# Attention-bias tables of an encoder layer: written whole to DRAM, or kept in place in SBUF

## The chip, the cores and the metric

One core of a Trainium2 chip runs the whole program. The metric is device time in microseconds (us) of one execution, the median of several runs. Engines are named as in the profile: PE (TensorE, matmuls) and PEld (its weight loads), DVE (VectorE), ACT (ScalarE), POOL (GpSimd), SP (SyncE, which here only issues transfers); "SPq" and "ACTq" are the transfers that SyncE and ScalarE issue.

## The reference

One encoder layer is applied to two inputs with the same weights: a sample of 1024 tokens and a prompt of 256. Width is 1024, the feed-forward width 2816, all in float32:

```python
x = x + 0.5 * rmsnorm(swiglu(rmsnorm(x, ffn1_pre), ffn1_w_gu, ffn1_w_down), ffn1_post)
h = rmsnorm(x, mix_pre)
qa, ka, va, qb, kb, vb = split(h @ w_in)
oa = window_gqa(rope(qa), rope(ka), va, sink_a)       # A: 8 heads, keys within 128 tokens
ob = neighbourhood_attn(qb, kb, vb, rpb_b)            # B: 8 heads on a (rows x 64) token grid
mix = concat([rmsnorm(oa, out_norm_a), rmsnorm(ob, out_norm_b)]) @ w_out
x = x + rmsnorm(mix, mix_post)
x = x + 0.5 * rmsnorm(swiglu(rmsnorm(x, ffn2_pre), ffn2_w_gu, ffn2_w_down), ffn2_post)
return rmsnorm(x, final_norm)
```

In `neighbourhood_attn` a query at row r and column c of the grid sees a window of at most 8 rows by 16 columns, clamped at the edges, and each score gets a learned bias `rpb[head, row difference, column difference]`; scores outside the window are set to -1e30 before the softmax.

## The kernel before, in words

**Order of the work.** The first feed-forward part is a gate-up phase (class `GateUp`) and a down phase (`Down`, `down_phase`); then come the mixer (`mix_attention`: input projection, attention A, attention B), the output projection (`MixOut`), and the second feed-forward part by the same two classes. Both feed-forward products use seven products of half-size operands instead of eight, so sums and differences of weights and of activations are formed beside the matmuls. Every float32 operand is split into a high and a low part (`split`, L65: ACT copies, DVE or POOL subtracts), and each product is three matmuls.

**Gate-up.** 22 blocks f of 128 hidden columns, in `GateUp.steps`. A block has 14 steps: seven products j for the first chunk of tokens (ch 0, 256 columns), seven for the second (ch 1, 384). PE works on a step while DVE and ACT take the step before out of PSUM (the tiles u, v, w, g) and split the next block's weights (`prep`). Results go to DRAM as planes w and v, stored by ACT. From block 11 on (`f >= HF`), the planes of block f - 11 are read back (`fetch`, tile `back`), and POOL forms four sums of old and new planes (`sums`, L328 to L338, tiles `back` and `sums`), which ACT stores. All stores are in ACT's queue, in the order written out by `queued`.

**Weights' sums.** `Down.weight_sums(i)` (L391) loads three blocks of `w_down`, forms four sums on POOL (L402 to L405, tiles `bx`, `bt`) and has ACT store them a block later. `block_hooks` puts it behind step 8 of a block; which block is told by its last argument. In the first feed-forward part that is block 1 and every even block (`f // 2 if f == 1 or f % 2 == 0`), in the second blocks 1 to 11 (`f - 1 if f <= HF`).

**Bias tables.** `bias_tables` (L518) prepares the bias of attention B in DRAM. `skew(g, tau)` puts the bias of four heads and one of three column cases tau in skewed form, with -1e30 outside the valid columns (tile `z`, POOL), and writes it to `zd` and `zp`. For the sample, `fill(a, rh)` then builds a full table `tt` out of it, from DRAM to DRAM: one transfer copies the valid band of 8 of 12 key rows for query row a and half rh, and one or two more fill the rest with the constant `neg`. For the prompt, `fill_neg` and `fill_p` build `ttp`. The list `first` (six skews, five fills) runs behind step 6 of gate-up blocks 2 to 10; the list `later` (eleven fills, four `fill_p`) is spread by `pinned` over the first three head groups of attention A, each behind the last half swap of the rope (`qs`) on SyncE's queue.

**Attention A.** Four head groups j, ten units t each (`att_A`): scores on PE (`s_ps`, out of the stacked rotated queries `stk`), a fused bias, mask and minimum on DVE (`bias_max`), exponentials on ACT, normalisation on POOL, transposes (`pt`) and the product with the values (`o_ps`) on PE, a fold on ACT and DVE into `st` (two buffers), and a store to `oAd` by SyncE. A unit's steps are spread over six steps of a software pipeline (`Pipe`, the lags in `ATT`), and the input projection of the next head group (L636, `pj`) is laid between them. Rope: ACT copies the projection (`qf`), SyncE swaps halves of its partitions (`qs`, four transfers of 32 partitions), POOL and DVE combine, and a split gives `stk`.

**Attention B.** Eight heads h, units n in the order 0, 3, 4, 1, 2 (4 is the prompt). `load_tab(h, tau)` (L857) loads a head's table: one transfer of 384 KB for tau 0 to 2 (tile `tab`, three buffers), two of 128 KB for the prompt (`tabp`). The first head's four are loaded ahead of the loop; the next head's are issued right behind the `bias_max` that read the buffer last. On SyncE's queue stand also the moves of keys to the other half of the partitions (L644, `stk`) and the loads of projection weights (L586, `mraw`), which the next heads need.

Of the kernel before, what the change touches and what calls it, by code (L numbers as in the profile page):

```python
# [19 lines left out]
NFF = FF // 128  # L20
# [146 lines left out]
class GateUp:  # L167
# [160 lines left out]
    def sums(self, f, ch):  # L328

        n, e, sub, add = CN[ch], self.c.nc.gpsimd.tensor_tensor, ALU.subtract, ALU.add  # L330
        x, y = self.back.pop((f, ch)), self.G.tile([128, 2 * n], F32, name="sums", tag=("ga", "gb")[ch], bufs=1)
        (w0, v0), (s3, s4) = [[z[:, :n], z[:, n:]] for z in (x, y)]
        w1, v1 = self.X["w"], self.X["v"]
        e(s3, w0, v0, op=sub)
        e(v0, v0, v1, op=add)
        e(w0, v0, w0, op=sub)
        e(s4, w1, w0, op=sub)
        return [lambda: self.store(("s2", "s1"), f, ch, x), lambda: self.store(("s3", "s4"), f, ch, y)]  # L338
# [41 lines left out]
class Down:  # L380
# [48 lines left out]
    def load_h(self, n):  # L429

        if n >= len(self.seq) or n in self.sub:
            return
        c, nc = self.c, self.c.nc
        q, p, m = self.seq[n]
        ch = 0 if p < CHUNKS[0][1] else 1
        k = len(PIECES[m])

        def tile(name):
            if n == 0:
                return self.G.tile([128, 6, 128], F32R, name=name, tag="x", bufs=3)[:, :k]  # L440
            return self.hp.tile([128, 6, 128], F32R, name=name, bufs=3)[:, :k]

        lo, hi = tile("hl"), tile("hh")
        g = next(g for g in PLANES if DOWN7[q][0] in g)
        src = self.hd[g][m][ch][g.index(DOWN7[q][0]) * CN[ch] // 128 + p - CHUNKS[ch][0]]
        self.last_h = nc.sync.dma_start(lo.bitcast(F32), src)
        split(c, hi, lo, lo.bitcast(F32))
        self.sub[n] = hi, lo
# [66 lines left out]
            self.cms.pop().__exit__(None, None, None)  # L515


def bias_tables(c, G, rpb, cmask, neg, tt, ttp, zd, zp):  # L518

    nc = c.nc
    def rows(g):
        rp = c.small.tile([96, 63], F32, name="rp", bufs=1)
        nc.gpsimd.memset(rp, 0.0)
        for h in range(4):
            nc.sync.dma_start(rp[h * 24 + 4:h * 24 + 19, 16:47], rpb[4 * g + h])
        nc.gpsimd.tensor_scalar(rp, rp, 8.0, None, op0=ALU.mult)
        return rp  # L530

    rps = {}

    def skew(g, tau):
        if tau == 0:
            rps[g] = rows(g)
        cm = G.tile([96, 16, 32], F32, name="cm", tag="t", bufs=2)
        nc.sync.dma_start(cm.rearrange("p q j -> p (q j)"), cmask[:, tau * 512:(tau + 1) * 512].to_broadcast([96, 512]))
        x = rps[g][:, 31 - 8 * tau:63 - 8 * tau]
        x = bass.AP(tensor=x.tensor, offset=x.offset, ap=[list(x.ap[0]), [-1, 16], [1, 32]])  # L540
        z = G.tile([96, 16, 32], F32, name="z", tag="t", bufs=2)
        nc.gpsimd.tensor_tensor(z, x, cm, op=ALU.add)
        for x in (zd[:, tau], zp[tau]):
            nc.sync.dma_start(x[:, 4 * g:4 * g + 4].rearrange("q h d j -> (h d) q j"), z)

    zf = zd.rearrange("q t h d j -> q (t h) (d j)")
    tf = tt.rearrange("t h a q r e j -> q (t h) a r (e j)")

    def fill(a, rh):
        e0 = min(a, 4) if rh else max(a - 4, 0)  # L550
        d0 = e0 - a - 4 * rh + 11
        nc.sync.dma_start(tf[:, :, a, rh, e0 * 32:e0 * 32 + 256], zf[:, :, d0 * 32:d0 * 32 + 256])
        for lo, hi in ((0, e0), (e0 + 8, 12)):
            if hi > lo:
                n = (hi - lo) * 32
                src = bass.AP(tensor=neg.tensor, offset=neg.offset, ap=[[0, 16], [0, 24], [1, n]])
                nc.sync.dma_start(tf[:, :, a, rh, lo * 32:hi * 32], src)

    def fill_p(a, n):
        nc.sync.dma_start(ttp[a, n, :, :, :, KC0[n]:KC0[n] + 32].rearrange("x h e j -> (x h) e j"),  # L560
                          zp[TAU[n], :, :, 11 - a:15 - a, :].rearrange("x h e j -> (x h) e j"))

    def fill_neg(a):
        nc.sync.dma_start(ttp[a].rearrange("n q h e k -> (n q h) (e k)"), neg.to_broadcast([512, 256]))

    first = [lambda tau=tau, g=g: (skew(g, tau), fill_neg(2 * g + tau - 1) if tau else None) for g in range(2) for tau in range(3)]
    first.append(lambda: fill(0, 0))
    fills = [lambda a=a, rh=rh: fill(a, rh) for a in range(8) for rh in range(2)][1:]
    while len(first) < HF - 2:
        two, fills = fills[:2], fills[2:]  # L570
        first.append(lambda two=two: [f() for f in two])
    return first, fills + [lambda a=a: [fill_p(a, n) for n in range(4)] for a in range(4)]

# [24 lines left out]
    return hi, lo, parts()  # L598


def mix_attention(c, tc, xt, w_in, sink, cosT, sinT, maskA, tt, ttp, oAd, oBd, mw, L, R,
                  close_left, open_out, late, mr, pre, fills):
    nc = c.nc
    xh, xl = xt
    pipe = c.pipe = Pipe()
# [96 lines left out]
    def rope(th, ps, store):  # L702
        n = TH[th][1]
        p0 = TH[th][0] % 1024
        qf = pa.tile([128, n], F32, name="qf", tag="qf", bufs=2)
        nc.scalar.activation(qf, ps, AF.Copy)
        qs = pa.tile([128, n], F32, name="qs", tag="qs", bufs=2)
        for b in range(4):
            state["pin"] = nc.sync.dma_start(qs[b * 32:b * 32 + 32], qf[(b ^ 1) * 32:(b ^ 1) * 32 + 32])
        yield  # L710
        nc.gpsimd.tensor_tensor(qf, qf, cos[:, p0:p0 + n], op=ALU.mult)
        nc.vector.tensor_tensor(qs, qs, sin[:, p0:p0 + n], op=ALU.mult)
        yield
        nc.vector.tensor_tensor(qf, qf, qs, op=ALU.add)
        yield
        store(th, qf, qs)
# [138 lines left out]
    tabs = {}  # L855

    def load_tab(h, tau):  # L857
        if h < 8:
            if tau < 3:
                T = pb.tile([128, 2, 384], F32, name="tab", bufs=3)  # L860
                nc.sync.dma_start(T.rearrange("p r x -> p (r x)"), tt[tau, h].rearrange("a q r e j -> (a q) (r e j)"))
            else:
                T = pb.tile([128, 2, 256], F32, name="tabp", bufs=1)
                for b in range(2):
                    nc.sync.dma_start(T[:, b], ttp[2 * b:2 * b + 2, :, :, h].rearrange("a n x e c -> (a n x) (e c)"))
            tabs[h, tau] = T

    def att_B(h, n, reload):

# [17 lines left out]
        rsum = c.small.tile([128, 2], F32, name="rsum")  # L887
        for i in range(2):
            bias_max(sbs[i], ps[i], tabs[h, tau][:, i, :], negm[:, i:i + 1], 3e38)
        if reload:  # L890
            load_tab(h + 1, tau)
        softmax_exp(sbs, negm, rsum)
        yield
        normalize(sbs, rsum)
        yield
        if n < 4:
# [62 lines left out]
                out.append((cost, lambda n=n, f=f: (load_to(n), f())))  # L959
        return out  # L960

    def pinned(f):
        with tc.issue_after(state["pin"].ins):
            f()

    with in_order(tc, mybir.EngineType.DVE):
        load_to(10)
        for i in (0, 16, 8):
# [9 lines left out]
    for j in range(4):  # L978
        units = [[(att_A(j, t), ATT)] for t in range(NT)]
        if j < 3:  # L980
            todo = P(("qA", j + 1))
            for n in range(7):
                if fills:
                    todo.insert(4 * n + 3, (0.0, lambda f=fills.pop(0): pinned(f)))
            pipe.run(units, todo)
        else:
            pipe.run(units + [[]] * 5, P(("qkB", 0), ("vB", 1)))
    R.close()
    pb = R.open("mixB", 1)
    for tau in (0, 2, 3, 1):  # L990
        load_tab(0, tau)
    during = [[("qkB", 1)], [("qkB", 2)], [("qkB", 3)], [("vB", 2), ("qkB", 4)], [("qkB", 5)], [("vB", 3), ("qkB", 6)], [("qkB", 7)]]
    for h in range(8):
        units = []
# [176 lines left out]
def encoder(tc, i, out_p, out_s):  # L1171
# [24 lines left out]
    oAd = dram.tile([4, 128, 1280], F32, name="oAd")  # L1196
    oBd = [dram.tile([4, 128, n], F32, name=f"oBd{n}") for n in (1024, 256)]
    zd = dram.tile([16, 3, 8, 24, 32], F32, name="zd")
    tt = dram.tile([3, 8, 8, 16, 2, 12, 32], F32, name="tt")
# [23 lines left out]
    def block_hooks(gu, f, extra, sums):  # L1223
# [19 lines left out]
        if f == NFF - 1:  # L1243
            for n, i in ((0, 0), (1, 1), (2, 2), (3, 3), (7, 4), (8, 5), (9, 6), (11, 7), (12, 8), (13, 9)):
                also(n, lambda i=i: d.load_w(0, i))
            also(12, lambda: d.load_h(0))
        return hooks

    def down_phase(gu, res, post, nxt, finish, last):
# [126 lines left out]
    for _ in nxt:  # L1376
        pass
    gu.load(2)
    late, later = bias_tables(c, G, i["rpb_b"][0], i["cmask"], i["neg"], tt, ttp, zd, zp)

    def behind():
        with tc.issue_after(gu.last_load.ins):
            late.pop(0)()

    for f in range(1, NFF):
        gu.run(f, block_hooks(gu, f, {6: behind} if 1 < f < HF else {}, f // 2 if f == 1 or f % 2 == 0 else None))
    L.close(2)
    R.close()
    state = dict(xn={}, late=[])
# [28 lines left out]
    def finish1(t, x, gain, halves, ss):  # L1418
# [7 lines left out]
        if "xt" in state:  # L1426
# [7 lines left out]
            else:  # L1434
# [9 lines left out]
    mix_attention(c, tc, state["xt"], i["w_in"][0], i["sink_a"], i["cosT"], i["sinT"], i["maskA"], tt, ttp, oAd, oBd,  # L1444
                  mw, L, R, lambda: L.close(4), mo.open, lambda: [list(x) for x in state["late"]], state["mr"], state["pre"], later)
    c.ps.use(y=(2, 3, 4, 5), tr=(6, 7, 0, 1))


# [127 lines left out]
```

## Time and profile before

| | |
|---|---|
| median of three runs | 2405.97 us (2403.55 to 2409.6) |
| the profiled execution | 2403.19 us, of which the span shown is 2401.4 |
| PE busy | 2273.8 us, 95% |
| DVE, ACT, POOL busy | 1458.6, 982.4, 709.0 us (61, 41, 30%) |
| mean granted TensorE clock | 0.977 |
| gate-up 1 / down 1 | about 20 to 610 / 610 to 890 us |
| attention A / attention B | about 959 to 1165 / 1170 to 1400 us |
| gate-up 2 / down 2 | about 1560 to 2113 / 2122 to 2390 us |

A line of the profile names engine, source line, operation, result tile and operands (`out<-in`). "Idle before" and the rows of the waits say what ended the time in which an engine stood still. A transfer's time to land runs from its issue to its last byte. The granted clock is the share of full speed that TensorE was given; below 1, the same matmuls take longer.

### The profile page before, as it was taken

What the parts mean: (1) busy time and instruction counts of PE and PEld (TensorE: products, weight loads), DVE (VectorE), ACT (ScalarE), POOL (GpSimd) and SP (SyncE); (2) the same over time, 40 slices, a digit from 0 to 9 for tenths busy, and PEclk for the clock granted to TensorE, in tenths of its full rate; (3) what the DMA queues carried; (4) which work ended last, traced back from release to release, by engine and by line L of the source; (5) the groups of instructions that cost most, each with busy time, mean ns of one, the idle gap of its engine ahead of it and who ended that gap; (6) DMA issues with size and microseconds to landing.
All of it is one profiled execution on the core that took longest, in us unless ns stands there. A gap on an engine that the chain in (4) does not pass through costs nothing. (4 is left out here: it accounts for less than half of the span.)

```text
span 2401.4 us, 36895 instructions
## 1 busy us (share of the span) xinstructions
PE 2273.8 (95%) x13328; PEld 2072.3 (86%) x13328; DVE 1458.6 (61%) x2575; ACT 982.4 (41%) x2043; POOL 709.0 (30%) x812
## 2 busy tenths in 40 slices
PE   6999999999999999878999989899999999999997
PEld 5999999999788787657898878789999999978876
DVE  7666656655545763548665656566666656544585
ACT  5322222222434543547665655342322222243454
POOL 6121125444000123436443334622213332300022
PEclk9999999999999999878999999899999999999999
DMA  4466656666656653334433445435455655555574
GB/s 135 119 155 158 153 144 195 188 184 185 208 188 192 221 184 107 73 77 85 111 106 93 123 156 176 155 114 164 139 172 157 185 145 159 149 189 183 191 230 157
DMA packets 417094, 372.47 MB, mean 155 GB/s; under 512 B 69200, under 2 KB 339408, under 8 KB 416912
## 3 DMA queue, kind: packets, MB, share of 16 engines
q1 hardware_dynamic: 286224, 278.87, 39.5%
q10 hardware_dynamic: 130688, 91.25, 12.4%
q8 instruction: 105, 1.72, 0.3%
q14 instruction: 77, 0.63, 0.1%
HBM read 249.85 MB, written 121.90 MB: 155 GB/s over the span
## 5 line engine op out<-in xcount | busy, mean ns | idle before, releaser
L280 PE MATMUL gups<-xh,ah 128*128 128x256 f32 (+1 forms) x2464 | 764.9, 311 | 18.6 <-DVE v L289 13.5
L280 PE MATMUL gups<-xh,al 128*128 128x256 f32 (+1 forms) x2464 | 762.1, 310 | 0.0
L280 PE MATMUL gups<-xl,ah 128*128 128x256 f32 (+1 forms) x2464 | 761.8, 309 | 0.0
L462 PE MATMUL dps<-wd,hh 128*128 128x512 f32 x1540 | 482.4, 394 | 7.9 <-ACT hh L69 7.9
L280 PEld LDWEIGHTS gups<-xh,ah 128*128 128x128 f32 x2464 | 466.7, 189 | 24.5 <-DVE v L289 15.8
L280 PEld LDWEIGHTS gups<-xl,ah 128*128 128x128 f32 x2464 | 467.3, 190 | 0.0
L280 PEld LDWEIGHTS gups<-xh,al 128*128 128x128 f32 x2464 | 466.9, 190 | 0.0
L462 PEld LDWEIGHTS dps<-wd,hh 128*128 128x128 f32 x1540 | 290.9, 189 | 70.3 <-ACT hh L69 9.8
L462 PE MATMUL dps<-wd,hl 128*128 128x512 f32 x770 | 304.2, 395 | 6.6 <-DVE hl L72 6.2
L69 ACT ACTIVATE ah<-s 128x512 fp32r<-128x512 f32 x176 | 111.3, 632 | 244.4 <-PE gups L280 165.9
L72 DVE TENSOR_TENSOR al<-s,ah 128x512 fp32r<-128x512 f32 x176 | 145.0, 824 | 98.1 <-ACT ah L69 97.4
L69 ACT ACTIVATE hh<-hl 128x768 fp32r<-128x768 f32 (+1 forms) x140 | 110.6, 791 | 209.6 <-DMA hl<-hd0s 55.3
L72 DVE TENSOR_TENSOR hl<-hl,hh 128x768 fp32r<-128x768 f32 (+1 forms) x140 | 124.6, 891 | 106.3 <-ACT hh L69 106.3
L462 PEld LDWEIGHTS dps<-wd,hl 128*128 128x128 f32 x770 | 145.8, 189 | 44.2 <-DVE hl L72 12.6
L659 POOL TENSOR_TENSOR sb<-sb,rc 128x384 f32<-128x384 f32 (+1 forms) x160 | 126.1, 810 | 158.0 <-DVE rc L657 144.3
L636 PE MATMUL pj<-xh,mh 128*128 128x512 f32 (+1 forms) x432 | 162.9, 378 | 0.3
L636 PE MATMUL pj<-xh,ml 128*128 128x512 f32 (+1 forms) x432 | 156.8, 363 | 0.1
L636 PE MATMUL pj<-xl,mh 128*128 128x512 f32 (+1 forms) x432 | 156.3, 362 | 0.0
L306 ACT ACTIVATE u<-u 128x256 f32<-128x256 f32 x88 | 41.5, 472 | 253.4 <-DVE u L289 208.9
L69 ACT ACTIVATE ah<-raw 128x512 fp32r<-128x512 f32 x132 | 83.4, 632 | 138.4 <-PE gups L280 131.5
L72 DVE TENSOR_TENSOR wd<-rawd,wd 128x512 fp32r<-128x512 f32 x154 | 106.2, 692 | 47.0 <-ACT wd L69 46.5
L162 POOL TENSOR_SCALAR rs<-ssq 128x1 f32<-128x1 f32 x20 | 12.5, 624 | 396.1 <-ACT junk L479 396.1
(183 smaller groups left out, 3680.4 us busy)
## 6 DMA issues: line engine op xcount, KB each, us to landing
raw<-in_ffn_w_gu_dram SPq DMA_DIRECT2D x88, 512.0 KB, 4.1
rawd<-in_ffn_w_down_dram SPq DMA_DIRECT2D x66, 256.0 KB, 3.3
bx<-in_ffn_w_down_dram SPq DMA_DIRECT2D x22, 512.0 KB, 5.1
bt<-in_ffn_w_down_dram SPq DMA_DIRECT2D x44, 256.0 KB, 4.8
rawd<-td0T SPq DMA_DIRECT2D x44, 256.0 KB, 3.2
rawd<-td1T SPq DMA_DIRECT2D x44, 256.0 KB, 3.2
tab<-tt SPq DMA_DIRECT2D x24, 384.0 KB, 3.8
hl<-hd0s SPq DMA_DIRECT2D x20, 384.0 KB, 3.2
```

The lines of the kernel that those rows point to most:

```text
L69: nc.scalar.activation(hi, src, AF.Copy)
L72: (lo_eng or nc.vector).tensor_tensor(lo, src, hi.bitcast(F32), op=ALU.subtract)
L162: nc.gpsimd.tensor_scalar(r, sums[0], sums[1] if len(sums) == 2 else 0.0, EPS, op0=ALU.add, op1=ALU.add)
L280: nc.tensor.matmul(ps, w[:, k, :], x[:, k, :], start=new and k == 0 and m == 0, stop=k == 3 and m == 2, skip_group_check=not new)
L306: self.last_act = nc.scalar.activation(X["u"], X["u"], AF.Silu)
L462: nc.tensor.matmul(ps, a[:, k, :], b, start=i == 0 and v == 0, stop=i == HF - 1 and v == 2)
L636: state["mm"] = nc.tensor.matmul(ps[:, :n], w[:, kk, :], xs[th][:, kk, :], start=first, stop=last)
L659: nc.gpsimd.tensor_tensor(s, s, rc[:, i:i + 1].to_broadcast(list(s.shape)), op=ALU.mult)
```

## The change

- The table `tt`, the function `fill` and all its transfers are removed, as is `pinned` with the fills in attention A. `bias_tables` returns one list of ten: six skews and the four `fill_p`, run behind step 6 of blocks 2 to 11.
- Attention B has three tiles `table`, one for each tau, which stay in place. POOL sets them to -1e30 once. `load_tab` writes only the valid bands, straight from `zd`: for each of eight query rows a and two halves rh, one transfer to 16 partitions with 1 KB each, so 16 transfers of 16 KB a table. It is a generator: the transfers of a = 0 to 3 are issued behind `bias_max`, those of a = 4 to 7 a pipeline step later, ahead of `normalize`. For head 0, the transfers with rh = 1 are issued by ACT; all others by SyncE.
- The first feed-forward part takes its weights' sums in blocks 1 to 11, like the second.
- Buffers: `cm` and `z` of the skew move from the slots `t` to `ga` and `gb`. The high half of the down phase's first operand (`hh` of `load_h(0)`) moves from slot `x` to `gb`, and `load_h(0)` from step 12 to step 10 of the last block; the last block's second `sums` tile moves from `gb` to `ga`. These three hold for both feed-forward parts.

```diff
     def sums(self, f, ch):
-        x, y = self.back.pop((f, ch)), self.G.tile(..., name="sums", tag=("ga", "gb")[ch], bufs=1)
+        x, y = self.back.pop((f, ch)), self.G.tile(..., name="sums", tag=("ga", "gb")[ch and f < NFF - 1], bufs=1)
...
         def tile(name):
             if n == 0:
-                return self.G.tile([128, 6, 128], F32R, name=name, tag="x", bufs=3)[:, :k]
+                t, b = ("x", 3) if name == "hl" else ("gb", 1)
+                return self.G.tile([128, 6, 128], F32R, name=name, tag=t, bufs=b)[:, :k]
...
-    first.append(lambda: fill(0, 0))
-    fills = [lambda a=a, rh=rh: fill(a, rh) for a in range(8) for rh in range(2)][1:]
-    while len(first) < HF - 2:
-        two, fills = fills[:2], fills[2:]
-        first.append(lambda two=two: [f() for f in two])
-    return first, fills + [lambda a=a: [fill_p(a, n) for n in range(4)] for a in range(4)]
+    return first + [lambda a=a: [fill_p(a, n) for n in range(4)] for a in range(4)]
...
     def load_tab(h, tau):
-        if h < 8:
-            if tau < 3:
-                T = pb.tile([128, 2, 384], F32, name="tab", bufs=3)
-                nc.sync.dma_start(T.rearrange("p r x -> p (r x)"), tt[tau, h].rearrange("a q r e j -> (a q) (r e j)"))
...
+        T = tabs[h, tau] = table[tau]
+        src = zd[:, tau, h].rearrange("q d j -> q (d j)")
+        for a in range(8):
+            if a == 4:
+                yield
+            for rh in range(2):
+                e0 = min(a, 4) if rh else max(a - 4, 0)
+                d0 = e0 - a - 4 * rh + 11
+                (nc.scalar if rh > h else nc.sync).dma_start(T[a * 16:a * 16 + 16, rh, e0 * 32:e0 * 32 + 256], src[:, d0 * 32:d0 * 32 + 256])
...
             bias_max(sbs[i], ps[i], tabs[h, tau][:, i, :], negm[:, i:i + 1], 3e38)
-        if reload:
-            load_tab(h + 1, tau)
+        load = load_tab(h + 1, tau) if reload else iter(())
+        next(load, None)
         softmax_exp(sbs, negm, rsum)
         yield
+        for _ in load:
+            pass
         normalize(sbs, rsum)
...
         if j < 3:
-            todo = P(("qA", j + 1))
-            for n in range(7):
-                if fills:
-                    todo.insert(4 * n + 3, (0.0, lambda f=fills.pop(0): pinned(f)))
-            pipe.run(units, todo)
+            pipe.run(units, P(("qA", j + 1)))
...
+    table = [pb.tile([128, 2, 384], F32, name=f"tab{x}", bufs=1) for x in range(3)]
+    for x in table:
+        nc.gpsimd.memset(x, NEG)
     for tau in (0, 2, 3, 1):
-        load_tab(0, tau)
+        for _ in load_tab(0, tau):
+            pass
...
-            also(12, lambda: d.load_h(0))
+            also(10, lambda: d.load_h(0))
...
-        gu.run(f, block_hooks(gu, f, {6: behind} if 1 < f < HF else {}, f // 2 if f == 1 or f % 2 == 0 else None))
+        gu.run(f, block_hooks(gu, f, {6: behind} if late and f > 1 else {}, f - 1 if f <= HF else None))
```

More of the change, by code (lines that the diff above doesn't have):

```diff
@@ L330, in sums @@
         n, e, sub, add = CN[ch], self.c.nc.gpsimd.tensor_tensor, ALU.subtract, ALU.add
-        x, y = self.back.pop((f, ch)), self.G.tile([128, 2 * n], F32, name="sums", tag=("ga", "gb")[ch], bufs=1)
+        x, y = self.back.pop((f, ch)), self.G.tile([128, 2 * n], F32, name="sums", tag=("ga", "gb")[ch and f < NFF - 1], bufs=1)
         (w0, v0), (s3, s4) = [[z[:, :n], z[:, n:]] for z in (x, y)]
@@ L515, in close, with bias_tables @@
             self.cms.pop().__exit__(None, None, None)
-def bias_tables(c, G, rpb, cmask, neg, tt, ttp, zd, zp):
+def bias_tables(c, G, rpb, cmask, neg, ttp, zd, zp):
     nc = c.nc
@@ L536, in skew @@
             rps[g] = rows(g)
-        cm = G.tile([96, 16, 32], F32, name="cm", tag="t", bufs=2)
+        cm = G.tile([96, 16, 32], F32, name="cm", tag="ga", bufs=1)
         nc.sync.dma_start(cm.rearrange("p q j -> p (q j)"), cmask[:, tau * 512:(tau + 1) * 512].to_broadcast([96, 512]))
@@ L540, in skew @@
         x = bass.AP(tensor=x.tensor, offset=x.offset, ap=[list(x.ap[0]), [-1, 16], [1, 32]])
-        z = G.tile([96, 16, 32], F32, name="z", tag="t", bufs=2)
+        z = G.tile([96, 16, 32], F32, name="z", tag="gb", bufs=1)
         nc.gpsimd.tensor_tensor(z, x, cm, op=ALU.add)
@@ L544, in skew @@
             nc.sync.dma_start(x[:, 4 * g:4 * g + 4].rearrange("q h d j -> (h d) q j"), z)
[L546 to L557, printed above, removed]
     def fill_p(a, n):
@@ L598, in split_win, with mix_attention @@
     return hi, lo, parts()
-def mix_attention(c, tc, xt, w_in, sink, cosT, sinT, maskA, tt, ttp, oAd, oBd, mw, L, R,
-                  close_left, open_out, late, mr, pre, fills):
+def mix_attention(c, tc, xt, w_in, sink, cosT, sinT, maskA, zd, ttp, oAd, oBd, mw, L, R,
+                  close_left, open_out, late, mr, pre):
     nc = c.nc
@@ L708, in rope @@
         for b in range(4):
-            state["pin"] = nc.sync.dma_start(qs[b * 32:b * 32 + 32], qf[(b ^ 1) * 32:(b ^ 1) * 32 + 32])
+            nc.sync.dma_start(qs[b * 32:b * 32 + 32], qf[(b ^ 1) * 32:(b ^ 1) * 32 + 32])
         yield
@@ L857, in load_tab @@
     def load_tab(h, tau):
-        if h < 8:
-            if tau < 3:
-                T = pb.tile([128, 2, 384], F32, name="tab", bufs=3)
-                nc.sync.dma_start(T.rearrange("p r x -> p (r x)"), tt[tau, h].rearrange("a q r e j -> (a q) (r e j)"))
[L862 to L865, printed above, removed]
-            tabs[h, tau] = T
+        if h >= 8:
+            return
+        if tau == 3:
+            T = pb.tile([128, 2, 256], F32, name="tabp", bufs=1)
+            for b in range(2):
+                nc.sync.dma_start(T[:, b], ttp[2 * b:2 * b + 2, :, :, h].rearrange("a n x e c -> (a n x) (e c)"))
+            tabs[h, tau] = T
+            return
+        T = tabs[h, tau] = table[tau]
[7 more added lines that the diff above has]
+                (nc.scalar if rh > h else nc.sync).dma_start(T[a * 16:a * 16 + 16, rh, e0 * 32:e0 * 32 + 256], src[:, d0 * 32:d0 * 32 + 256])
     def att_B(h, n, reload):
@@ L960, in P @@
         return out
-    def pinned(f):
-        with tc.issue_after(state["pin"].ins):
-            f()
     with in_order(tc, mybir.EngineType.DVE):
@@ L1198, in encoder @@
     zd = dram.tile([16, 3, 8, 24, 32], F32, name="zd")
-    tt = dram.tile([3, 8, 8, 16, 2, 12, 32], F32, name="tt")
     zp = dram.tile([3, 16, 8, 24, 32], F32, name="zp")
@@ L1378, in encoder @@
     gu.load(2)
-    late, later = bias_tables(c, G, i["rpb_b"][0], i["cmask"], i["neg"], tt, ttp, zd, zp)
+    late = bias_tables(c, G, i["rpb_b"][0], i["cmask"], i["neg"], ttp, zd, zp)
     def behind():
@@ L1443, in encoder @@
     c.ps.use(pj=(0, 1), s=(2, 3), t=(4, 5), o=(6, 7), y=(0, 1), tr=(6, 7))
-    mix_attention(c, tc, state["xt"], i["w_in"][0], i["sink_a"], i["cosT"], i["sinT"], i["maskA"], tt, ttp, oAd, oBd,
-                  mw, L, R, lambda: L.close(4), mo.open, lambda: [list(x) for x in state["late"]], state["mr"], state["pre"], later)
+    mix_attention(c, tc, state["xt"], i["w_in"][0], i["sink_a"], i["cosT"], i["sinT"], i["maskA"], zd, ttp, oAd, oBd,
+                  mw, L, R, lambda: L.close(4), mo.open, lambda: [list(x) for x in state["late"]], state["mr"], state["pre"])
     c.ps.use(y=(2, 3, 4, 5), tr=(6, 7, 0, 1))
```

## The prediction

> **What bounds the kernel now.** I read the page first (busy shares and the forty slices), then the stretches by stage, then who TensorE waited for in the stages with holes, then the transfers and SyncE's waits there.
>
> ```profile
> PE 2273.8 (95%) x13328; PEld 2072.3 (86%) x13328; DVE 1458.6 (61%) x2575; ACT 982.4 (41%) x2043; POOL 709.0 (30%) x812
> PE   6999999999999999878999989899999999999997
> PEclk9999999999999999878999999899999999999999
> ```
>
> TensorE is busy 95% of the span: a change can only remove its holes and the time it runs at a lowered clock, or add some. The one deep hole, in busy time and in clock, is at slices 17 to 19, which is attention A. By stage (columns: stretch, its length, busy of PE, PEld, DVE, ACT, POOL, granted clock, DMA share, GB/s):
>
> ```profile
> 100.00:350.00 250.00, 249.19 (x1710) 248.57 (x1709) 149.78 (x248) 67.03 (x128) 43.39 (x35) 1.00 0.60 154
> 350.00:607.00 257.00, 244.45 (x1652) 241.21 (x1650) 158.08 (x250) 69.36 (x134) 113.98 (x99) 0.99 0.65 187
> 959.00:997.00 38.00, 33.51 (x184) 28.47 (x184) 26.32 (x78) 25.68 (x70) 23.96 (x41) 0.91 0.30 66
> 997.00:1064.00 67.00, 45.65 (x210) 35.84 (x210) 31.61 (x90) 28.59 (x76) 21.79 (x41) 0.76 0.33 78
> 1064.00:1118.00 54.00, 44.34 (x220) 36.91 (x221) 34.36 (x92) 31.11 (x83) 23.65 (x43) 0.82 0.40 86
> 1118.00:1154.00 36.00, 35.11 (x226) 29.75 (x225) 32.78 (x98) 32.35 (x94) 26.69 (x51) 1.00 0.35 76
> 1160.00:1180.00 20.00, 20.00 (x115) 17.42 (x114) 9.23 (x26) 9.30 (x25) 6.35 (x8) 1.00 0.53 162
> 1170.00:1372.00 202.00, 201.35 (x1262) 180.45 (x1261) 127.62 (x346) 125.72 (x332) 73.66 (x98) 1.00 0.38 102
> 1600.00:1850.00 250.00, 250.00 (x1713) 250.00 (x1712) 157.99 (x255) 69.46 (x131) 59.95 (x42) 1.00 0.48 154
> 1850.00:2100.00 250.00, 250.00 (x1704) 249.67 (x1704) 150.54 (x255) 71.02 (x135) 86.09 (x85) 1.00 0.57 160
> ```
>
> Rows 3 to 6 are the four head groups j of attention A: 38, 67, 54 and 36 us for the same ten units each. Rows 1 and 2 are the halves of the first gate-up phase, the last two those of the second, which has no hole at all. Attention B (row 8) is full.
>
> **Attention A: the fills go.** Before, eleven table fills (each one copy of 384 KB and one or two fills with the constant) and four prompt fills are put into j = 0 to 2, on SyncE's queue, between the rope's half swaps (qs) and the output stores (oAd). The change takes the table fills out of the program and puts the prompt fills into gate-up blocks 8 to 11. Who TensorE waited for in j = 0 to 2, the transfers of j = 1 and then of j = 3 (last column: median us to landing), and one of SyncE's own waits:
>
> ```profile
> PE o_ps L792 <- DVE st L687: 14.2, 8, 3.6
> PE s_ps L665 <- DVE stk L72: 12.9, 7, 3.3
> ...
> oAd<-st SPq DMA_DIRECT2D x10, 64.0 KB, 7.1
> qs<-qf SPq DMA_DIRECT2D x8, 64.0 KB, 8.9
> ...
> oAd<-st SPq DMA_DIRECT2D x11, 64.0 KB, 2.2
> qs<-qf SPq DMA_DIRECT2D x1, 32.0 KB, 1.9
> ...
> SPq L799 <- DMA tt<-in_neg_dram: 4.0, 2, 3.0
> ```
>
> The reader is to see both ways in which a fill hurts. The store of `st` takes 7.1 us beside fills and 2.2 without; `st` has two buffers, so the fold waits and o_ps behind it. The half swap takes 8.9 against 1.9, so the rotated queries (stk) come late for s_ps. And SyncE stands still for a landing fill, with which store and swap share no data. Each hole then lowers the granted clock (0.76, 0.82), so the work itself stretches. The work alone is busy time by clock: 33.51 x 0.91 + 45.65 x 0.76 + 44.34 x 0.82 = 101.5 us of 159. The bounds of the gain are therefore 27 us (the first two waits, nothing else) and 57 (all idle, all clock). I take the pace of j = 3, the same code with no fill beside it: 3 x 36 = 108, a gain of **51**. It is nearer to the upper bound because DVE (31 to 34 us a group) and ACT (29 to 31) also fit in 36. Next to be late there is DVE.
>
> **First gate-up: weights' sums.** Six of the eleven weight sums (each four POOL operations) lie in blocks 1 to 10 and five in blocks 12 to 20, beside the planes' sums, also on POOL. After, all are in blocks 1 to 11, as in the second gate-up.
>
> ```profile
> PE gups L280 <- DVE v L289: 11.5, 8, 2.1
> ...
> ACT ah L69 <- POOL sums L337: 18.3, 5, 5.0
> ...
> 467.50 1.74 POOL L404 TENSOR_TENSOR bx<-bt,bx 128x512 f32<-128x512 f32 x1
> ...
> 471.61 0.74 POOL L337 TENSOR_TENSOR sums<-w,back 128x256 f32<-128x256 f32 x1
> ...
> 472.38 0.37 ACTq L319 DMA_DIRECT2D hd0s<-sums  x1
> 472.85 0.63 ACT L69 ACTIVATE ah<-s 128x512 fp32r<-128x512 f32 x1 [5.50 <-PE gups L280]
> ```
>
> The chain: weight sums (L404 is one) sit between the planes' sums (L337) on POOL, the store of the planes' sums (hd0s) waits at the head of ACT's queue until 472.38, ACT has stood 5.50 us when its next split starts (the row names TensorE, which had long been done), DVE's evacuation behind that split is late, TensorE stops. The hole of this half is 257 - 244.45 = 12.6 us; the second gate-up's same half, with no weight sums in it but for block 11, has none. Gain **12**, bounds 10 and 13. The cover in the first half: the second gate-up has a weight sum in every block at PE 250.00 of 250 and POOL 60. Here six skews come on top (before too) and four prompt fills of four transfers. I cost them at nothing; if that cover failed, the 0.8 us that this half idles now is the nearest row. The skew's new buffers (ga, gb) are last used before block 1. The hidden tile of the down phase's first load (hh, now in gb, hook 10) starts ACT's split earlier, but the hole at that seam is:
>
> ```profile
> PE dps L462 <- ACT hh L69: 2.3, 1, 2.3
> ...
> PE dps L462 <- ACT hh L69: 5.6, 1, 5.6
> ...
> 2117.20 0.99 POOL L337 TENSOR_TENSOR sums<-w,back 128x384 f32<-128x384 f32 x1
> 2118.21 0.82 SPq L446 DMA_DIRECT2D hl<-hd1w  x2
> ```
>
> The next load goes out when POOL's last sum ends, which the change doesn't move. Zero, bounds -3 and +3 (the last sum's buffer now waits for a store half a block older).
>
> **Attention B: 384 small transfers for 24 large.** Each table load (one 384 KB transfer) becomes sixteen of 16 KB. The first three tables cost three POOL memsets, 24 issues on SyncE and 24 on ACT; the other 21 cost 336 issues on SyncE, eight behind the bias step, eight a step later. The next head's k moves (stk) and weight loads (mraw) queue behind them. No row shows a 16-partition load, so its price goes by the nearest (issue time min/median/max in ns; then pairs in the order of time, us):
>
> ```profile
> L865 SPq DMA_DIRECT2D tabp<-ttp x14: 319/382/1112, 1179.9 to 1360.6; - x14
> L644 SPq DMA_DIRECT2D stk<-stk x42: 461/467/1171, 1177.0 to 1371.3; - x42
> L586 SPq DMA_DIRECT2D mraw<-in_w_in_dram x10: 383/538/723, 1170.7 to 1283.8; - x10
> ...
> 961.22 2.42 SPq L709 DMA_DIRECT2D qs<-qf  x4
> ...
> 1179.92 0.80 SPq L865 DMA_DIRECT2D tabp<-ttp  x2
> ...
> 1204.78 1.49 SPq L865 DMA_DIRECT2D tabp<-ttp  x2
> ...
> tabp<-ttp SPq DMA_DIRECT2D x14, 128.0 KB, 2.5
> ```
>
> From 0.40 us each (tabp: plain rows of 1 KB out of DRAM, as these are) to 0.605 (qs: few partitions). At 0.40: 336 x 0.40 = 134, plus what stays (42 x 0.467 + 10 x 0.538 + 14 x 0.382 = 30) is 164 of 202 us: SyncE fills 81% and TensorE's matmuls hide it. The shortest heads last 24.9 us (tabp to tabp) and take 48 x 0.40 + 5 = 24: just covered. At the start, 26 issues stand where 5 stood: 21 x 0.40 = 8.4 us; ACT's 24 (10 us) fit into its idle 10.7 of 20 at 1160. Half of the 8.4 shows: **+4**. At 0.605: 203 + 30 - 202 = 31, plus 21 x 0.605 = 13: **+44**. Below zero is excluded: TensorE idles 0.65 us there. I take +4, since tabp has source, rows and direction in common.
>
> The Trainium skill, "DMA: Bandwidth & Descriptors", section "Rules for kernel authors", speaks against this part: small transfers should be coalesced, and under 64 KB one pays mostly overhead. The page's "Anatomy of one DMA" puts that overhead at about 2.0 us a transfer (on the gpsimd path); paid one after the other, 336 of them would be an estimated 672 us, where the stage has 202. The trace agrees on the latency (tabp lands in 2.5 us), not on the sum: its pairs go out 0.40 us apart.
>
> **Sum.** 2403.2 (profiled execution) - 51 - 12 + 4 = 2344. The median of the runs is 2.8 above that execution, so 2347.
>
> **Rivals.** (1) In attention A only the direct waits go (27), the rest being the in-order chain of rope and softmax: for it, j = 2 took 54 us although its transfers were mostly the short prompt fills; against it, j = 3. 2371. (2) SyncE binds in attention B at 0.605 us: for it, all its few-partition rows; 2387. (3) Slower: the small loads don't overlap, SyncE waits for landings. It decides from 0.66 us an issue (357 x 0.66 - 172 = 63, the whole gain); at 0.70, 2421. Against it, SyncE issued six fills in 3.2 us that took 11.9 to land:
>
> ```profile
> 963.68 0.59 SPq L552 DMA_DIRECT2D tt<-zd  x1
> ...
> 966.30 0.62 SPq L557 DMA_DIRECT2D tt<-in_neg_dram  x1
> ...
> tt<-zd SPq DMA_DIRECT2D x4, 384.0 KB, 11.9
> ```
>
> With six in flight and tabp's 2.5 us to land, 0.42 is the limit. Rival 3 is what the skill's rule on small transfers would look like here.
>
> **How the numbers follow.** Forecast 0.65 (its own range 2333 to 2362); rival 1 0.16; rival 2 0.13; rival 3 0.04; 0.02 for a near tie. The range 2330 to 2382 holds forecast, rival 1 and part of rival 2. Under 0.3% (7 us) a measurement can't tell from no change: faster 0.94, same 0.02, slower 0.04.
>
> **What would show it.** Right: j = 0 to 2 at 34 to 38 us each, qs and oAd landing in about 2 us, clock near 1.00; 350 to 607 without waits of gups for v; 48 short issues a head on SyncE, 0.32 to 0.42 us each. Wrong: s_ps waiting for stk or ACT for mraw in attention B, SyncE without a gap there, ACT's exp late at its start, or j = 1 and 2 still above 45 us.

## The result: a gain of 22 us where 59 were forecast

| | before | changed |
|---|---|---|
| median of five runs | 2405.97 us (2402.64 to 2413.55) | 2384.09 us (2380.05 to 2390.71) |
| profiled execution / its span | 2403.19 / 2401.4 us | 2382.16 / 2380.4 us |

The ratio is 0.9907, 95% interval 0.9881 to 0.9933: faster, but 2384 lies just outside the range of 2330 to 2382. The page of the changed kernel, the same three lines as were shown of before:

```profile
PE 2265.4 (95%) x13328; PEld 2066.6 (87%) x13328; DVE 1457.8 (61%) x2575; ACT 980.4 (41%) x2043; POOL 713.0 (30%) x815
PE   6989999999999999999999899799999999989997
PEclk9999999999999999999999899899999999999999
```

The deep hole of slices 17 to 19 is gone. In its place PE has a dent in slice 3, early in the first gate-up phase, and one with a lowered clock at slice 23, the end of attention B. To put numbers on them, here are the rows of the timeline at which each part of the work begins, first of before (gate-up block 12, down phase, first projection, attention A, attention B, second gate-up), then of the changed kernel. The first column is the start in us.

```profile
346.94 0.28 PE L280 MATMUL gups<-xh,ah 128*128 128x256 f32 x1
...
609.80 1.05 PE L462 MATMUL dps<-wd,hh 128*128 128x512 f32 x2
...
892.18 0.48 PE L636 MATMUL pj<-xh,mh 128*128 128x512 f32 x1
...
959.10 0.50 PE L665 MATMUL s_ps<-kA,stk 128*128 128x256 f32 x2 [2.14 <-DVE stk L72]
...
1170.04 0.88 PE L665 MATMUL s_ps<-stk 128*128 128x384 f32 x4
...
1544.67 0.28 PE L280 MATMUL gups<-xh,ah 128*128 128x256 f32 x1
```

```profile
370.15 0.28 PE L280 MATMUL gups<-xh,ah 128*128 128x256 f32 x1
...
615.83 0.62 PE L463 MATMUL dps<-wd,hh 128*128 128x512 f32 x2
...
902.56 0.48 PE L619 MATMUL pj<-xh,mh 128*128 128x512 f32 x1
...
970.00 0.50 PE L648 MATMUL s_ps<-kA,stk 128*128 128x256 f32 x2 [2.14 <-DVE stk L72]
...
1121.93 0.88 PE L648 MATMUL s_ps<-stk 128*128 128x384 f32 x4
...
1521.95 0.28 PE L280 MATMUL gups<-xh,ah 128*128 128x256 f32 x1
```

Each row's lag against the same row of before, and its difference from the row ahead, gives the account:

| part | forecast | measured |
|---|---|---|
| gate-up 1 up to block 12 | 0 | **+23.2** |
| gate-up 1 from block 12 to the first down product | -12 | -17.2 |
| down 1 to the first projection | 0 | +4.4 |
| projection ahead of attention A | 0 | +0.5 |
| attention A | -51 | **-59.0** |
| attention B and output projection | +4 | **+25.4** |
| second feed-forward part | 0 | +1.7 |
| sum | -59 | -21.0 |

(Attention B and the output projection stand together, because the last units of the one run beside the first products of the other.) Two terms of the sum had the right place and came out larger than forecast, by 5 and by 8 us; that hides a part of the misses in the total. Two terms were wrong by 23 and by 21 us the other way. The stretches of the changed kernel, in the columns known from before; below them from block 12 to the first down product, and attention B with the output projection, each first before and then changed:

```profile
100.00:350.00 250.00, 235.06 (x1565) 233.79 (x1564) 153.98 (x234) 63.83 (x122) 66.44 (x47) 0.97 0.64 171
...
970.00:1004.00 34.00, 32.35 (x197) 28.09 (x198) 31.59 (x89) 28.34 (x79) 25.03 (x40) 0.95 0.23 51
1004.00:1038.00 34.00, 33.09 (x219) 29.29 (x218) 31.52 (x93) 29.69 (x84) 26.99 (x49) 1.00 0.24 55
...
1122.00:1366.00 244.00, 227.96 (x1345) 195.24 (x1343) 143.06 (x386) 140.91 (x370) 83.38 (x110) 0.97 0.40 89
```

```profile
346.94:609.80 262.86, 249.82 (x1681) 246.28 (x1681) 162.41 (x256) 71.52 (x137) 114.46 (x100) 0.99 0.64 185
370.15:615.83 245.68, 245.27 (x1682) 244.51 (x1681) 142.82 (x248) 70.46 (x133) 79.50 (x80) 1.00 0.57 159
...
1170.04:1544.67 374.63, 360.26 (x2077) 314.38 (x2076) 232.56 (x512) 218.38 (x510) 151.73 (x173) 0.98 0.43 133
1121.93:1521.95 400.02, 374.12 (x2077) 318.73 (x2076) 234.13 (x512) 220.14 (x514) 153.00 (x176) 0.96 0.44 118
```

The second half of gate-up 1 is full, as forecast. In the first half PE did 1565 matmuls in the 250 us that held 1710: it idles 14.9 us, and at a granted clock of 0.97 the work itself takes about 7.5 us longer (an estimate, 0.03 of 250). Attention A now runs at 34 us a head group. Attention B, which had been full, stands still for 16 of 244 us. Counted with the output projection, the idle time grows by 11.5 us (25.9 against 14.4), and the same 2077 matmuls are busy for 13.9 us longer, at a clock of 0.96 in place of 0.98.

**Where the first half lost its time.** Waits of the first 350 us of the changed kernel, and the time its skews' stores took to land (last column); then the same two stores before:

```profile
PE gups L280 <- ACT u L292: 14.9, 4, 4.4
...
ACT ah L69 <- DMA zd<-z: 23.0, 4, 6.1
...
zd<-z SPq DMA_DIRECT2D x6, 192.0 KB, 11.7
zp<-z SPq DMA_DIRECT2D x6, 192.0 KB, 12.5
```

```profile
zd<-z SPq DMA_DIRECT2D x6, 192.0 KB, 3.6
zp<-z SPq DMA_DIRECT2D x6, 192.0 KB, 5.5
```

Four times ACT stands still, 23.0 us in all, and four times PE waits for it. One of the four places in the timeline:

```profile
130.68 0.33 SPq L545 DMA_DIRECT2D zd<-z  x1
131.05 3.97 SPq L545 DMA_DIRECT2D zp<-z  x1
...
131.69 2.28 ACTq L406 DMA_DIRECT2D td0T<-bt  x1
...
136.54 0.33 ACTq L406 DMA_DIRECT2D td0T<-bt  x1
...
142.47 0.38 ACTq L319 DMA_DIRECT2D hd0w<-w  x1
142.90 0.63 ACT L69 ACTIVATE ah<-s 128x512 fp32r<-128x512 f32 x1 [5.32 <-DMA zd<-z]
```

The two stores of a skew (SyncE) and the three stores of the weights' sums (ACT; the first and the last are shown) go out within 6 us of each other. ACT's next plane store, `hd0w<-w`, shares no data with `zd`, but ACT comes past it only when `zd` has landed, 11.8 us after its issue, and the split behind it (`ah`) is late. In the built program the transfers of SyncE and ACT take eight completion semaphores in turn, and a transfer waits for the one eight ahead of it; here that is `zd` (in the trace, `zd<-z` and `hd0w<-w` both carry semaphore 105).

**Where attention B lost its time.** Transfers of the bands (their issue time min/median/max in ns), and SyncE's timeline at the start of the stage:

```profile
L859 SPq DMA_DIRECT2D tab<-zd x360: 302/418/1957, 1118.7 to 1356.9; - x180
...
L859 ACTq DMA_DIRECT2D tab<-zd x24: 309/432/981, 1116.6 to 1129.6; - x24
```

```profile
1118.72 16.01 SPq L859 DMA_DIRECT2D tab<-zd  x33
...
1136.62 11.79 SPq L859 DMA_DIRECT2D tab<-zd  x22
...
1165.91 11.23 SPq L859 DMA_DIRECT2D tab<-zd  x24
```

One issue takes 0.42 us, but they stand 0.47 to 0.54 us apart (11.23 / 24, 11.79 / 22). Over the stage SyncE's 360 take 187.6 us with their gaps, and hardly anything is free: from 1115 to 1366 us the gaps of over 0.3 us between its issues add up to 12.6 us (to 176 in the 240 us from 1160 of the kernel before). The next head's keys and weights come when the bands let them through.

### The profile page after: what moved, and what is told of

It reads as the page before. It is cut to its first block, busy times and chain, and to the rows that moved or that the text cites. A ratio compares the mean times of both kernels' runs of the same rounds, so it can differ in the third digit from the quotient of the medians.

```text
span 2380.4 us, 37317 instructions
## 1 busy us (share of the span) xinstructions
PE 2265.4 (95%) x13328; PEld 2066.6 (87%) x13328; DVE 1457.8 (61%) x2575; ACT 980.4 (41%) x2043; POOL 713.0 (30%) x815
## 3 DMA queue, kind: packets, MB, share of 16 engines
q10 hardware_dynamic: 131456, 91.64, 12.6%
## 5 line engine op out<-in xcount | busy, mean ns | idle before, releaser
L280 PE MATMUL gups<-xh,ah 128*128 128x256 f32 (+1 forms) x2464 | 766.8, 311 | 20.4 <-ACT u L292 14.9
L72 DVE TENSOR_TENSOR al<-s,ah 128x512 fp32r<-128x512 f32 x176 | 139.6, 793 | 107.2 <-ACT ah L69 106.5
```

What stands on the lines that cost most here:

```text
L72: (lo_eng or nc.vector).tensor_tensor(lo, src, hi.bitcast(F32), op=ALU.subtract)
L280: nc.tensor.matmul(ps, w[:, k, :], x[:, k, :], start=new and k == 0 and m == 0, stop=k == 3 and m == 2, skip_group_check=not new)
```

## The experiments

All times are medians; the gain is counted against the changed kernel's 2384. The kernel before, run again beside each group of experiments, had medians of 2403.3 to 2407.5 us, so differences of up to 4 us say nothing, and the ratios are the safer comparison. Lags and parts are each read from one profiled execution.

### 1. Which transfer stands eight behind (a_lane, a_lane4)

```diff
         for x in (zd[:, tau], zp[tau]):
             nc.sync.dma_start(x[:, 4 * g:4 * g + 4]..., z)
+        nc.sync.dma_start(c.extra[g, tau:tau + 1], z[0:1, 0])     # a_lane; in a_lane4 only if tau > 0
```

> One transfer of 128 bytes is added behind each of the six skews' two stores, nothing else. Theory (shared ring): SyncE's and ACT's transfers take eight completion semaphores in turn, and hd0w<-w stands on ACT's queue exactly eight behind zd<-z in the blocks of skews 2, 3, 5 and 6, so ACT stands still until the slow zd has landed; these are the four steps of 5 to 6 us that gate-up 1 lost (23.0 in all). By the order of this program the store stands eight behind zd in the blocks of skews 1 and 4 instead: two stalls, at those two places, 11.5 us, so 2384 - 11.5 = 2372. Rival (crowding: the skews' stores and the weights' sums' stores simply share the DMA engines, whatever the order): the four stalls stay where they are, 2384 to 2386.

> The same added transfer of 128 bytes, but only behind skews 2, 3, 5 and 6. Shared ring: no hd0w<-w stands eight behind a zd any more; the 23 us are gone but for 0 to 3, ACT has no wait for zd, 2361 to 2364, although a transfer more is issued. Crowding: 2384 to 2386, as every byte is still moved.

Measured: a_lane 2373.7, a_lane4 2376.1. The number came true for a_lane, the theory did not. ACT's wait for `zd` is gone in both, but up to block 12 they still lose 17.1 and 17.8 us instead of 23.2, in the blocks where it was lost before. ACT waits for other transfers, here in a_lane:

```profile
ACT u L306 <- DMA td0T<-bt: 26.1, 4, 7.7
...
ACT ah L69 <- DMA zp<-z: 7.5, 2, 3.9
```

The ring of eight decides which transfer ACT is seen to wait for. In these two it is worth about 6 us at block 12, and even that is not sure: four kernels with the changed kernel's code in this phase (b_two, b_pairs, b_split and e_seam, below) lag by 18.9 to 25.7 us there. The rest has another cause. (`c.extra` is a scratch tile in DRAM.)

### 2. The weights' sums alone (p_sums)

The kernel before, with the sums in blocks 1 to 11 and nothing else changed:

```diff
-    ... f // 2 if f == 1 or f % 2 == 0 else None))
+    ... f - 1 if f <= HF else None))
```

> The kernel before with one part of the change alone: the weights' sums in blocks 1 to 11; skews, table fills, attention as before. Shared ring: by this program's order no hd0w<-w stands eight behind a zd, so the first half loses nothing and the second half gains its 12: 2406 - 12 = 2394. Rival (the sums in every block beside a skew are the cost, for POOL or the DMA engines): 2406 - 12 + 23 = 2417.

Measured: 2406.1, a ratio to before of 0.9995 (0.9986 to 1.0005): neither of the two. Up to block 12 it loses 17.1 us, but only 5.5 of them by the end of the skews' blocks; most of the rest falls in blocks 8 to 11, where this kernel still has its table fills. In the skews' blocks it keeps the buffers of before. That pointed at the new ones.

### 3. Small pieces, blocks and buffers (a_rows, a_skew_late, a_tags, a_sums_back)

```diff
-        for x in (zd[:, tau], zp[tau]):                                     # a_rows
-            nc.sync.dma_start(x[:, 4 * g:4 * g + 4].rearrange("q h d j -> (h d) q j"), z)
+        for x in (zd, zp):      # rows r to r + 96 of a flat view with 512 columns
+            nc.sync.dma_start(x...[r:r + 96], z.rearrange("p q j -> p (q j)"))
...
-    {6: behind} if late and f > 1 else {}                                   # a_skew_late
+    {6: behind} if late and f > HF else {}                                  # (cm and z also as in a_tags)
...
-        cm = G.tile(..., tag="ga", bufs=1); z = G.tile(..., tag="gb", bufs=1)      # a_tags
+        cm = G.tile(..., tag="t", bufs=2); z = G.tile(..., tag="t", bufs=2)
...
-    f - 1 if f <= HF else None                                              # a_sums_back
+    f // 2 if f == 1 or f % 2 == 0 else None
```

> Each skew's two stores write the same 192 KB as 96 rows of 2 KB in place of 1536 pieces of 128 bytes; the order of all transfers stays. The values of the bias land in other places, so the bias added is not the reference's. Theory (small pieces: 3072 of them a skew hold the DMA engines for about 12 us, and whichever transfer stands behind them on ACT's queue is late): zd and zp land in under 4 us, the 23 us of gate-up 1's first half go down to 0 to 5, 2361 to 2366. Rival (volume: the weights' sums' 2 MB a block beside the block's other traffic): 15 us or more stay, 2376 or above.

> The six skews go to blocks 12 to 17 (behind the last weights' sums) and the prompt fills to blocks 18 to 21; mask and z use the weights' sums' two free buffers again. Theory (skews beside weights' sums): the first half loses nothing, 23 us back; the second half, which has 128 KB fetches and planes' sums in its blocks, may lose 0 to 8: 2361 to 2369. Rival (the skews' stores delay whatever stands beside them): the loss moves to the second half whole, 2380 to 2386.

> The changed kernel with the mask and z of the skews in the weights' sums' two buffers again, as before the change; all else as changed. Theory (the new buffers, which the prediction took as free, let mask, z and the two stores go out beside the weights' sums' stores; in the old ones the mask waits until those have landed): gate-up 1's first half loses about 6 as in the skews' blocks of the kernel before with the sums alone, not 23: 2384 - 17 = 2367. Rival (the buffers don't matter): 2382 to 2386.

> The changed kernel with the weights' sums on the schedule of before (six in blocks 1 to 10, five in blocks 12 to 20); the skews keep their new buffers. Theory (skew and weights' sums in one block are what crowds): every other block of the first half is free of sums, its loss falls to 0 to 6, and the hole of 12 in the second half comes back: 2384 - 20 + 12 = 2376. Rival (the skews in their new buffers cost it alone): 23 stay and 12 come: 2396.

| | median | ratio to before | lag at block 12 |
|---|---|---|---|
| changed kernel | 2384.1 | 0.9907 (0.9881 to 0.9933) | +23.2 |
| a_rows | 2359.1 | 0.9812 (0.9790 to 0.9834) | +2.9 |
| a_skew_late | 2361.7 | 0.9824 (0.9804 to 0.9843) | -0.1 |
| a_tags | 2363.8 | 0.9824 (0.9806 to 0.9841) | +8.3 |
| a_sums_back | 2373.6 | 0.9864 (0.9844 to 0.9884) | +0.4 |

All four rivals fall. The skews' stores cost their time as 3072 pieces of 128 bytes beside the weights' sums: as rows the same bytes in the same order lose almost nothing, though the stores land in 7.7 and 8.4 us, not in under 4 as expected. With the skews in other blocks there is no loss at all, and with the sums in every other block none either (the hole of the second half is back there). A wait of a_tags, and the landing of its skews' store, say what the old buffers did:

```profile
SPq L539 <- DMA td0T<-bt: 66.1, 6, 13.7
...
zd<-z SPq DMA_DIRECT2D x6, 192.0 KB, 3.3
```

L539 loads the mask `cm`. In the shared buffers it must wait until the weights' store has landed, so the skew comes later, and its stores go out apart from the weights' (in one place of a_tags, the weights' stores at 131.8 to 133.8 us and `zd` at 143.5). The collision over a buffer was a throttle that kept two bursts apart; the change took it away. The 8 us that a_tags still loses were not taken apart; 3.8 of them fall in block 8, beside the first prompt fill. With the skews moved behind the sums (a_skew_late) the first half is full, and the second, which now has them, idles 3.1 us:

```profile
100.00:350.00 250.00, 250.00 (x1721) 249.76 (x1720) 163.50 (x258) 71.08 (x134) 64.41 (x46) 1.00 0.52 162
350.00:595.00 245.00, 241.86 (x1653) 240.82 (x1652) 139.84 (x244) 67.89 (x130) 89.15 (x88) 1.00 0.74 184
```

### 4. How attention B pays (b_two, b_pairs, b_split)

```diff
-        for a in range(8):                                                  # b_two
-            ...
-            for rh in range(2):
-                (nc.scalar if rh > h else nc.sync).dma_start(T[a * 16:a * 16 + 16, rh, e0 * 32:e0 * 32 + 256], src[:, ...])
+        for rh in range(2):       # one transfer to all 128 partitions, 1 KB each
+            (nc.scalar if rh > h else nc.sync).dma_start(T[:, rh, 0:256], ...)
...
+            t = bass.AP(..., ap=[<16 partitions>, [384 + (e0 - e1) * 32, 2], [1, 256]])   # b_pairs: both bands of row a,
+            x = bass.AP(..., ap=[<16 rows of zd>, [(e0 - e1 + 4) * 32, 2], [1, 256]])     # rh = 1 first, e0 and e1 for rh = 0, 1
+            (nc.scalar if a % 2 > h else nc.sync).dma_start(t, x)
...
-                (nc.scalar if rh > h else nc.sync).dma_start(...)           # b_split
+                (nc.scalar if rh else nc.sync).dma_start(...)
```

> The changed kernel with each table loaded by two transfers of 128 KB in place of sixteen of 16 KB; the same bytes land, but every band at the table's left edge and from row offsets that rise, so the bias added is not the reference's. Theory (SyncE's issue time): attention B and the output projection get back what they lost, 25 us between them, less 2 to 4 for the 42 large loads: 2384 - 22 = 2362; SyncE with idle stretches in attention B. Rival (the tables in place: a load waits for the last reader of its one buffer, and DVE waits for the load): 2378 to 2384, DVE's and ACT's waits for tab stay.

> The two halves of a table change places, so that one transfer carries both bands of one query row: 8 transfers of 32 KB a table in place of 16 of 16 KB; all else as in the changed kernel. Theory (price by the issue, 0.49 us apart on SyncE): 192 issues fewer, 94 us of SyncE's time; attention B with the output projection within 6 us of the run with two loads a table (373): 2354 to 2361. Rival (price by the 1 KB pieces, whose number stays): 2380 to 2386.

> Sixteen transfers of 16 KB a table as in the changed kernel, but for every head the eight of the second half go out on ACT's queue. Theory (the issues fill SyncE): SyncE has half of them, 168 issues or 82 us fewer, ACT's 168 more at 0.43 us are 72 us for an engine that is 62% busy in this stage; attention B gets back most of its loss unless ACT becomes the bound: 2357 to 2372. Rival (the count of transfers in flight, eight for both queues together, is what binds): 2380 to 2388.

| | median | ratio to before | attention B and output projection |
|---|---|---|---|
| before | | | 374.6 |
| changed kernel | 2384.1 | 0.9907 | 400.0 |
| b_two | 2354.1 | 0.9779 (0.9763 to 0.9795) | 373.1 |
| b_pairs | 2354.6 | 0.9785 (0.9765 to 0.9804) | 371.2 |
| b_split | 2372.2 | 0.9873 (0.9860 to 0.9887) | 397.3 |

With two loads a table the whole loss is gone, so tables in place cost nothing. With eight it is gone too, at the same number of 1 KB pieces: the price goes by the issue. The band transfers of b_pairs, SyncE's longest wait there, and the stage:

```profile
L861 SPq DMA_DIRECT2D tab<-zd x180: 302/422/1778, 1123.6 to 1332.7; - x180
```

```profile
SPq L627 <- ACT stk L69: 29.2, 15, 3.1
```

```profile
1126.00:1342.00 216.00, 212.88 (x1336) 189.66 (x1334) 139.86 (x382) 139.26 (x369) 83.97 (x110) 1.00 0.41 100
```

Twice the bytes take the same 0.42 us to issue, and SyncE waits 29.2 us for the keys (`stk`) instead of letting them wait. In b_split the total fell to the upper end of what was expected, but by luck: this stage regained only 2.7 us; 5.4 came from the first gate-up phase, whose code is the same and whose crowded half happened to end sooner. ACT's exponentials tell why; the row of b_split, then that of the changed kernel:

```profile
L635 ACT ACTIVATE sb<-sb,negm 128x384 f32<-128x384 f32 (+3 forms) x160 | 92.3, 579 | 76.4 <-DMA tab<-zd 49.5 <-DVE negm L631 18.9 <-DMA stk<-stk 3.2
```

```profile
L635 ACT ACTIVATE sb<-sb,negm 128x384 f32<-128x384 f32 (+3 forms) x160 | 92.3, 579 | 32.1 <-DVE negm L631 30.9
```

Moved to ACT's queue, the issues stand in front of the work of an engine that TensorE waits for: in the stage, 29 exponentials come directly behind 106 issues, and ACT has idled 57.8 us ahead of them, 0.55 us an issue. The price is about the same, only another engine pays it. Whether the ring of eight, which both queues share, adds to it was not tested, so this run alone does not exclude its rival; b_two and b_pairs do not need it.

### 5. The seam at the down phase (e_seam)

```diff
-                t, b = ("x", 3) if name == "hl" else ("gb", 1)
+                t, b = "x", 3
-            also(10, lambda: d.load_h(0))
+            also(12, lambda: d.load_h(0))
```

(and the planes' sums in their old buffers.)

> The changed kernel with the down phase's first hidden tile as before: hh in the buffers it had, its load at step 12 of the last block, the planes' sums in their old buffers. With the weights' sums alone in blocks 1 to 11 (no change here) the seam fell by 9 us against before, in the changed kernel by 3. Theory (the new place of hh gives that back): the seam gains 5, 2379. Rival (nothing, as predicted for this part): 2382 to 2386.

Measured: 2370.9, ratio 0.9858 (0.9841 to 0.9875), a gain of 13, more than either side gave. The part from the first down product to the first projection takes 279.4 us in place of 286.7; that is the seam. It repeats: the ten kernels here with the hidden tile in its new place take 284.8 to 287.1 us for this part, e_seam and best (below) 279.4 and 279.6. Attention B with the output projection takes 3.2 us less, and why is open. Waits around the seam, the changed kernel and then e_seam:

```profile
PE dps L463 <- ACT hh L69: 4.8, 1, 4.8
...
ACT hh L69 <- DMA hl<-hd0w: 21.1, 8, 6.7
```

```profile
PE dps L462 <- ACT hh L69: 1.1, 1, 1.1
...
ACT hh L69 <- DMA hl<-hd0w: 6.2, 5, 2.4
```

Two steps earlier, the split of the hidden tile stands at the head of ACT's queue while its data is still on the way; the splits of the down weights wait behind it, and with them SyncE's loads into their buffers (SyncE waits 28.6 us for those splits around the seam, in e_seam 25.9). This chain is read from the waits; the three parts of the edit (the tile's buffer, the step of its load, the buffers of the planes' sums) were not run one by one.

### 6. The repairs together (best)

a_skew_late, e_seam and b_pairs in one kernel.

> The three repairs together: skews in blocks 12 to 17 and prompt fills behind them, the hidden tile's load as before, one transfer for two bands. If the three losses lie in separate stretches, their gains against the changed kernel add: 22.4 + 13.2 + 29.5 = 65, so 2319, which is the 2347 forecast less the terms that had been taken as unavoidable. Rival (they overlap: what one frees another had already hidden, in the seam above all): 2330 to 2340.

Measured: 2325.5 (2323.0 to 2332.4), ratio to before 0.9678 (0.9664 to 0.9692); against the changed kernel this is a gain of 59, where the three single gains make 65. They add but for 6 us; by the ratios it is 55 against 61, again 6 apart. The time lies between the two sides, 6.5 us above the first and 4.5 below the rival's range. Part by part, in the profiled executions, the repairs do add: the first half gives back 23.2 us (a_skew_late alone 23.3), the seam 7.1 (e_seam 7.3), attention B with the output projection 28.5 (b_pairs 28.8), and the second half costs 4.1 (a_skew_late 2.9). What does not come again is the part of e_seam's gain that fell outside the seam. Its page has no dent left where the two losses were:

```profile
PE   6999999999999999999999999899999999989997
...
PEclk9999999999999999999999999999999999999999
```

## Why the prediction was wrong, step by step

Two steps failed: that the first half of gate-up would lose nothing, and that SyncE's issues in attention B would stay hidden behind TensorE's matmuls. A third thing runs through the sum: outside attention A it prices a hole by its idle time alone, and in the rows above the longer busy time at a lowered clock comes on top.

- **Attention A, -51: right, measured -59.** The four head groups take about 34 us each (they begin at 970, 1002, 1036 and 1069 us). The 59 lie 2 us beyond the upper bound of 57, which left out j = 3; that group too takes 34 in place of 36. The reasons held too: the half swap lands in 2.0 us and the store in 2.1, and of the waits of o_ps for st nothing is left. The pace of j = 3, 36 us, was still a little slow as a measure. Rival 1 (only the direct waits go) falls.

```profile
PE s_ps L648 <- DVE stk L72: 3.1, 2, 2.1
...
oAd<-st SPq DMA_DIRECT2D x35, 64.0 KB, 2.1
qs<-qf SPq DMA_DIRECT2D x24, 64.0 KB, 2.0
```

- **Gate-up, second half, -12: the place right, the size too small.** The 17.2 us are beyond the bounds of 10 and 13. The idle time came out as forecast: from block 12 to the first down product it was 13.0 us before and is 0.4 now, 12.6 less. The other 4.6 us are busy time (249.82 against 245.27 for the same work), partly the lowered clock of 0.99, which the sum put at nothing. The last 4.9 of the 17.2 us fall in the last six gate-up steps, and they too belong to the weights' sums: p_sums and e_seam, with the old load of the hidden tile, gain 5.1 there, and a_sums_back, with the new load and the old schedule of the sums, loses 0.7.
- **Gate-up, first half, 0: the first step that failed, measured +23.2.** "The second gate-up has a weight sum in every block at PE 250.00 of 250" was a cover for POOL's work and for the bytes, and it held for both: a_skew_late does the same with PE at 250.00. But the second gate-up has no skews. The step counted the skews as there before too, and took their new buffers as free because nothing else used them. What it missed is that the old buffers had kept the skews' small pieces apart from the weights' stores (with them, a_tags gets back 15 of the 23 us) and that the sums now stood in each of the skews' blocks (with the old schedule, a_sums_back gets back all of it). The 0.8 us taken as the nearest row was a row of a stage without that overlap.
- **Attention B, +4: the second step that failed, measured +25.4, inside its bounds.** The count of issues was right, their price too small, and they do not stay hidden. The price was taken from one pair (tabp, 0.40 us from one issue to the next); the second pair that the prediction shows gives 0.75 us by the same reckoning (1.49 for two). In rows of 22 to 33 the band transfers stand 0.47 to 0.54 us apart, 0.52 over the stage. SyncE, which was to be 81% full, has hardly a gap left, and so TensorE's matmuls no longer hide it. Put into the prediction's own sum, 0.52 gives 336 x 0.52 + 30 - 202 = 3, plus 21 x 0.52 = 11 at the start, 14 together. That is near the 11.5 us by which the idle time grew; the 13.9 us of longer busy time were no term of the sum. Rival 2, that SyncE binds, was right about the place, at somewhat over half its price (25 of 44). The sign "SyncE without a gap" had been named. In rival 3, the rows show five fills in 3.2 us, not six, so its limit would be 0.50 and not 0.42; the outcome does not hang on it.
- **The seam, 0 with bounds of 3: wrong, +4.4 in the down phase.** The earlier split of the hidden tile brought nothing and cost 7.3 us there against e_seam. The prediction looked at the wait for that tile alone; what it missed is, by the waits, what stands behind that split on ACT's queue.
- **The rule of the Trainium skill on small transfers** ("DMA: Bandwidth & Descriptors", section "Rules for kernel authors": coalesce them) pointed the right way, and the weight that the prediction gave the trace instead was right only on the size: 336 issues at 0.52 us are 175 us, not the estimated 672 of the fixed cost paid each time, but with the start's and all other issues that is what fills the stage. b_pairs, which follows the rule by half, takes all of the loss away.

## What to carry to other kernels

A buffer shared by two streams is also a throttle: when you give one of them its own, ask which bursts will now go out together, and on which in-order queue the late one will be waited for. Price a run of small transfers by their spacing in a long run and by issues, not by a pair, and look for the cheapest merge first: halving the count was worth as much here as dividing it by eight. A wait that the profile puts on one transfer may be only the slot it came by; move that slot, and if the wait moves to another transfer, the cause is the crowd.

## What the runs showed of the hardware that was not expected

- Small pieces are slow beside others: 192 KB in 1536 pieces of 128 bytes (`zd`, median) landed in 3.3 to 3.6 us where they went out apart from the weights' stores (a_tags, p_sums, before), in 11.7 beside them (changed kernel); as 96 rows of 2 KB in 7.7 beside them (a_rows).
- The issue of a band transfer takes the same 0.42 us (median) with 16 KB (changed kernel) and with 32 KB (b_pairs), and 0.62 us with 128 KB to 128 partitions (b_two).
- The crowded half of gate-up does not repeat to the microsecond: with the same code in this phase its first down product came at 615.8, 612.0, 618.8 and 610.4 us (changed kernel, b_two, b_pairs, b_split).
